# A hybrid encoder block: another way to build the row of c, a first scaled sum moved, the last quarters of two projections by token tile, the FFN input by blocks

## The chip, the cores and the metric

The kernel runs on one core of a Trainium2 chip. The metric is device time in microseconds (us) of one execution; lower is better. The core has a matrix engine (TensorE, PE in the profile; PEld is its weight load), a vector engine (DVE), a scalar engine (ACT), GpSimd (POOL) and SyncE (SP), which here only issues transfers. Each engine works through its own list of instructions in order. The lists are made ahead of time by a planner, which goes by program order as a priority, knows which instruction needs which, and hands out the buffers of a tag in program order; instructions wrapped in `order(...)` keep their written order on their engine whatever the planner would like better.

## What is computed

One layer on 256 tokens of width 2048, followed by an RMSNorm. The parts around the change:

```python
c_act = jax.nn.silu(c)
mod = c_act @ ada_w + ada_b
shift_m, scale_m, gate_m, shift_f, scale_f, gate_f = jnp.split(mod[:, None, :], 6, axis=-1)
h = rms_norm(x, norm_mix_w) * (1 + scale_m) + shift_m
proj = h @ w_in
...
x = x + gate_m * ((g_a * y_a + g_b * y_b) @ w_out)
hf = rms_norm(x, norm_ffn_w) * (1 + scale_f) + shift_f
gt, up = jnp.split(hf @ w_gate_up, 2, axis=-1)
x = x + gate_f * ((jax.nn.silu(gt) * up) @ w_down)
return rms_norm(x, norm_final_w)
```

Between the two lie a bidirectional mLSTM and a bidirectional gated delta rule, which the change leaves alone.

## The kernel before

All weights are streamed once from HBM in tiles of 1 MB, 128 partitions by 8 KB, into the tag `raw` of pool `st`, which has three buffers. Products of full precision are made from halves: `wh` is the weight rounded to the matmul's format (a copy on ACT, L165), `wl` the rest (a subtraction on DVE, L166), each with three buffers, and each product is three matmuls: high by high, low by high, high by low (L181 to L183).

**The opening.** `c` comes as one line of 8 KB; four row matmuls against ones spread it over the 128 partitions, and ACT takes its Silu into `row_c` (L100, L101). `cst` (which holds the identity, `ident`) and `pk` are loaded behind it on ACT's queue. The two token tiles `xt0` and `xt1` of x come on SP's queue, into the tag `ra` with five buffers, of which a third is taken by `junk`, the unused output of ACT's sums of squares (L417). 32 transposes on PE, in eight banks of four, turn x into feature blocks; DVE copies each bank (L424). Then sixteen blocks follow in a loop. Block b loads `ra0`, `ra1` (rows of the modulation weights, for scale and shift) and `raw` (input weights for sixteen output groups), in this order on SP. DVE multiplies `ra0` by `row_c` and sums it (L443), scales x with the sum and with `rows`, the tokens' reciprocal norms (L444), sums `ra1` likewise (L445); ACT adds that sum as a bias (L446) and rounds to `hh` (L447), DVE makes `hl` one block later (L450), and PE runs sixteen products of 256 columns (L452), of two passes each.

**The projections.** `tjob` runs a product by token tiles: chunks of four k blocks in halves of two; for each k block it serves token tile 0 and then 1, so both accumulators end together. `o` (output projection of the mixer) has four column groups of four chunks each, `d` (down projection) four groups of eleven chunks. When a group ends, `residual` multiplies by the gate row and adds to `x1` on DVE (L1008, L1009), and ACT sums the squares (L1010).

**The other modulation parts** are summed in the background: `ada_part` loads a 1 MB tile on SP, also into `raw`, and DVE multiplies and sums it (L110). `pump()`, called once per chunk, takes one such step at every second call in `o` (`every[0]`), every fourth in the FFN; `sums(P)` empties the list. Behind `o` it finishes part 4, which the FFN input needs.

**The FFN input.** `token_rstd` makes the reciprocal norms (L1014 to L1016). For each of four column quarters DVE scales both token tiles (`xn`, L1043), PE transposes (L1050), DVE applies scale and shift from PSUM (`hf`, L1052), and ACT and DVE split into `hfh` and `hfl`, two feature blocks at a time (L205, L206). Then eleven column groups run a gate job, an up job, and transposes of their product into `ffh` and `ffl`.

**The end.** After `d`, `token_rstd` again, then DVE scales x1 by token and by the final weight `nf` (L1092), group by group, each followed by its store on SP (L1093).

## Time and profile before

| | |
|---|---|
| runs | 2104.91, 2110.9, 2117.63 us; median 2110.9 |
| profiled execution | 2114.43 us, its span from first to last instruction 2112.6 us |
| mean granted TensorE clock | 0.984 |
| transfers | 485.64 MB, mean 230 GB/s |
| opening, to the end of its last block of products on PE | 0 to about 139 us |
| `o`, last quarter's last matmul | starts at 1345.58 us |
| gate, first matmul | starts at 1357.65 us |
| `d`, last matmul | starts at 2097.65 us |

A row of the timeline gives start and length in us, the engine (a q behind its name: its queue or sequencer), the line of the kernel, the operation, the tile written and the tiles read, the shape and a count if several were merged. In brackets stands how long the engine sat idle before it and which engine's instruction, or which transfer, ended that. A row of a window gives its length, the busy time of PE, PEld, DVE, ACT and POOL with instruction counts, the clock granted to PE as a share, the busy share of the transfer engines and GB/s. Matmuls are pipelined: one of 512 columns is shown with 0.39 us and starts 0.23 us after the one before.

### The profile page before, as it was taken

What the parts mean: (1) busy time and instruction counts of PE and PEld (TensorE: products, weight loads), DVE (VectorE), ACT (ScalarE), POOL (GpSimd) and SP (SyncE); (2) the same over time, 40 slices, a digit from 0 to 9 for tenths busy, and PEclk for the clock granted to TensorE, in tenths of its full rate; (3) what the DMA queues carried; (4) which work ended last, traced back from release to release, by engine and by line L of the source; (5) the groups of instructions that cost most, each with busy time, mean ns of one, the idle gap of its engine ahead of it and who ended that gap; (6) DMA issues with size and microseconds to landing.
All of it is one profiled execution on the core that took longest, in us unless ns stands there. A gap on an engine that the chain in (4) does not pass through costs nothing.

```text
span 2112.6 us, 26903 instructions
## 1 busy us (share of the span) xinstructions
PE 2034.2 (96%) x10374; PEld 1704.1 (81%) x10374; DVE 1403.3 (66%) x2065; ACT 1041.7 (49%) x1545; POOL 76.7 (4%) x149
## 2 busy tenths in 40 slices
PE   8999999989999899999999999899999999999997
PEld 6877779967988798888777878678888888878885
DVE  6788767776886687765677777765656654454454
ACT  2147557745773677555443444344444444444442
POOL 0002100100010000000000000000000000000000
PEclk9999999999999999999999999899999999999999
DMA  9976664456566656577986677666666665555553
GB/s 393 421 316 173 185 224 154 149 172 229 193 205 198 223 196 218 186 252 250 343 324 248 241 299 280 234 219 234 241 239 222 240 218 192 187 199 195 187 195 120
DMA packets 81075, 485.64 MB, mean 230 GB/s; under 512 B 9881, under 2 KB 19361, under 8 KB 26545
## 3 DMA queue, kind: packets, MB, share of 16 engines
q1 hardware_dynamic: 68672, 459.34, 60.3%
q0 software_dynamic: 4960, 9.49, 2.7%
q10 hardware_dynamic: 7314, 15.10, 1.9%
q8 instruction: 81, 1.33, 0.2%
q14 instruction: 48, 0.39, 0.1%
HBM read 467.07 MB, written 16.82 MB: 229 GB/s over the span
## 4 chain that ended last, share of the span: by engine, by line
PE 76%; DVE 8%; DMA 8%; issue 5%; ACT 3%; POOL 0%; SPq 0%; DVEq 0%; ACTq 0%; POOLq 0%
PE acc_up L183 4%; PE acc_up L181 4%; PE acc_up L182 4%; PE acc_d L181 4%; PE acc_d L182 4%; PE acc_d L183 4%; PE acc_gt L181 4%; PE acc_gt L182 4%; PE acc_gt L183 4%; PE first L452 3%; PE acc_b L145 2%; PE acc_b L147 2%; PE acc_b L146 2%; PE acc_o L181 2%; PE acc_o L182 2%
## 5 line engine op out<-in xcount | busy, mean ns | idle before, releaser
L166 DVE TENSOR_TENSOR wl_d<-raw_d,wh_d 128x1024 fp32r<-128x1024 f32 x88 | 107.8, 1225 | 123.2 <-ACT wh_d L165 123.2
L166 DVE TENSOR_TENSOR wl_up<-raw_up,wh_up 128x1024 fp32r<-128x1024 f32 x88 | 107.8, 1225 | 111.7 <-ACT wh_up L165 111.7
L110 DVE SCALAR_TENSOR_TENSOR ada<-ada,crow 128x2048 f32<-128x2048 f32 x64 | 146.3, 2286 | 43.8 <-DMA ada<-ada 43.4
L145 PE MATMUL acc_b<-hh,wh_b 128*128 128x256 f32 x576 | 163.8, 284 | 0.0
L147 PE MATMUL acc_b<-hh,wl_b 128*128 128x256 f32 x576 | 161.1, 280 | 1.8 <-DVE wl_b L142 1.8
L166 DVE TENSOR_TENSOR wl_gt<-raw_gt,wh_gt 128x1024 fp32r<-128x1024 f32 x88 | 107.1, 1224 | 83.7 <-ACT wh_gt L165 83.7
L165 ACT ACTIVATE wh_d<-raw_d 128x1024 fp32r<-128x1024 f32 x88 | 93.3, 1061 | 138.9 <-PE acc_d L182 134.0
L146 PE MATMUL acc_b<-hl,wh_b 128*128 128x256 f32 x576 | 160.2, 278 | 0.0
L165 ACT ACTIVATE wh_gt<-raw_gt 128x1024 fp32r<-128x1024 f32 x88 | 93.2, 1060 | 135.2 <-PE acc_gt L182 78.4
L165 ACT ACTIVATE wh_up<-raw_up 128x1024 fp32r<-128x1024 f32 x88 | 93.3, 1060 | 117.8 <-PE acc_up L182 84.7
L181 PE MATMUL acc_gt<-wh_gt,hfh 128*128 128x512 f32 x352 | 138.6, 397 | 2.9 <-ACT hfh L205 2.7
L182 PE MATMUL acc_gt<-wh_gt,hfl 128*128 128x512 f32 x352 | 139.3, 396 | 0.0
L183 PE MATMUL acc_gt<-wl_gt,hfh 128*128 128x512 f32 x352 | 138.5, 393 | 0.0
L181 PE MATMUL acc_d<-wh_d,ffh 128*128 128x512 f32 x352 | 137.5, 391 | 0.0
L182 PE MATMUL acc_d<-wh_d,ffl 128*128 128x512 f32 x352 | 137.5, 391 | 0.0
L183 PE MATMUL acc_d<-wl_d,ffh 128*128 128x512 f32 x352 | 137.0, 389 | 0.0
L181 PE MATMUL acc_up<-wh_up,hfh 128*128 128x512 f32 x352 | 137.0, 389 | 0.0
L183 PE MATMUL acc_up<-wl_up,hfh 128*128 128x512 f32 x352 | 137.0, 389 | 0.0
L182 PE MATMUL acc_up<-wh_up,hfl 128*128 128x512 f32 x352 | 137.0, 389 | 0.0
L452 PE MATMUL first<-x,raw 128*128 128x256 f32 x512 | 114.6, 386 | 6.6 <-ACT x L446 6.6
L452 PEld LDWEIGHTS first<-x,raw 128*128 128x128 f32 x512 | 98.3, 193 | 22.9 <-ACT x L446 9.4
L147 PEld LDWEIGHTS acc_b<-hh,wl_b 128*128 128x128 f32 x576 | 108.6, 189 | 2.2 <-DVE wl_b L142 2.2
(344 smaller groups left out, 5245.2 us busy)
## 6 DMA issues: line engine op xcount, KB each, us to landing
ada<-ada SPq DMA_DIRECT2D x64, 1024.0 KB, 4.9
raw_gt<-wgu SPq DMA_DIRECT2D x44, 1024.0 KB, 4.9
raw_up<-wgu SPq DMA_DIRECT2D x44, 1024.0 KB, 4.9
raw_d<-wd SPq DMA_DIRECT2D x44, 1024.0 KB, 4.8
raw_b<-winb SPq DMA_DIRECT2D x36, 1024.0 KB, 4.9
ra<-ada SPq DMA_DIRECT2D x32, 1025.0 KB, 14.6
raw<-win SPq DMA_DIRECT2D x16, 1024.0 KB, 12.7
raw_z<-wint SPq DMA_DIRECT2D x16, 1024.0 KB, 5.2
```

Of the source, the lines that this page charges most:

```text
L110: V.scalar_tensor_tensor(raw, raw, 1.0, row_c[:, :D], ALU.mult, ALU.mult, accum_out=mod[:, c0 + b : c0 + b + 1])
L145: PE.matmul(o, wh[:, k], hh[:, kk], start=kk == 0, stop=False)
L146: PE.matmul(o, wh[:, k], hl[:, kk], start=False, stop=False)
L147: PE.matmul(o, wl[:, k], hh[:, kk], start=False, stop=kk == KB - 1)
L165: order(S.activation(wh, raws[u][:, k0 : k0 + 2], AF.Copy), early)
L166: order(V.tensor_tensor(wl, raws[u][:, k0 : k0 + 2], wh.bitcast(F32), ALU.subtract), early)
L181: PE.matmul(ps[t], xh[:, kk, c], wh[:, k], start=kk == 0, stop=False)
L182: PE.matmul(ps[t], xl[:, kk, c], wh[:, k], start=False, stop=False)
L183: PE.matmul(ps[t], xh[:, kk, c], wl[:, k], start=False, stop=kk == last)
L452: PE.matmul(first[o], raw[:, o], x[:, b], start=b == 0 and o % 2 == 0, stop=b == KB - 1 and o % 2 == 1)
```

## The change

The row of c: `c` is loaded feature by partition (128 lines of 16 numbers), Silu is taken there, each of sixteen columns is spread over a tile of ones on DVE, transposed on PE and copied from PSUM by DVE. `junk` moves into `hl`. The loads of a block become a function and put `raw` ahead of the two `ra` from block 1 on; the first scaled sum of block 0 stands behind the first copy of x; ACT takes every second copy. `tjob` gets `last_by_token`: its last chunk runs all products of token tile 0, then of 1, with `done` called after each. The last groups of `o` and `d` use it, with their residuals in forced order. The background sums and an early square root (`root`, whose result nobody reads) come before the last group of `o`; another such root before the last group of `d`. The first gate job is a generator that is advanced from inside the last `o` group (its first half of weights) and from inside the FFN input, which now goes block by block. In `d`, the product with `nf` is taken group by group for the first three groups, and the last scaling is shared by DVE and ACT.

```diff
-    c1 = st.tile([1, D], F32, tag="raw", bufs=3, name="c1")
-    S.dma_start(c1, crow.unsqueeze(0))
+    cR = st.tile([P, KB, P], F32, tag="raw", bufs=3, name="cR")
+    S.dma_start(cF, crow)
...
+    order(S.activation(cF, cF, AF.Silu))
     for g in range(4):
         pc_ = acc_ps.tile([P, 512], F32, tag="acc", name=f"crow{g}")
-        PE.matmul(pc_, ones[0:1], c1[:, g * 512 : (g + 1) * 512], start=True, stop=True)
-        S.activation(row_c[:, g * 512 : (g + 1) * 512], pc_, AF.Silu)
+        for e in range(4):
+            b = 4 * g + e
+            order(V.tensor_scalar(cR[:, b], ones, cF[:, b : b + 1], None, ALU.mult))
+            order(PE.transpose(pc_[:, e * P : (e + 1) * P], cR[:, b], ident))
+        order(V.tensor_copy(row_c[:, g * 512 : (g + 1) * 512], pc_))
...
         todo = [(u, k0) for u in range(len(chunks)) for k0 in (0, 2)]
-        made = [halves(*q) for q in todo[:early]]
-        if early:
-            yield True
+        made = []
+        for i, q in enumerate(todo[:early]):
+            made.append(halves(*q))
+            if steps > 1 or i == early - 1:
+                yield True
...
+        if last_by_token:
+            w = [halves(len(chunks) - 1, k0) for k0 in (0, 2)]
+            for t in range(2):
+                c = slice(t * P, (t + 1) * P)
+                for k in range(4):
...
+                done(t, ps[t])
+                yield True
...
-        junk = w0.tile([P, D + 2], F32, tag="ra", bufs=5, name="junk")
+        junk = hl.rearrange("p b t -> p (b t)")[:, :D]
...
+        def loads(b):
+            ra = [w0.tile([P, D + 2], F32, tag="ra", bufs=5, name=f"ra{b}_{i}") for i in range(2)]
+            raw = st.tile([P, N0, P], F32, tag="raw", bufs=3, name=f"raw0_{b}")
+            if b:
+                order(nc.sync.dma_start(raw, win0[b]))
+            for i in range(2):
+                order(nc.sync.dma_start(ra[i], ada2[b, :, i]))
+            if not b:
+                order(nc.sync.dma_start(raw, win0[b]))
+            return ra, raw
...
-            V.tensor_copy(x[:, 2 * b2 : 2 * b2 + 2], px.rearrange("p (e t) -> p e t", e=2))
+            if b2 % 2:
+                order(S.activation(x[:, 2 * b2 : 2 * b2 + 2], pe_, AF.Copy))
+            else:
+                order(V.tensor_copy(x[:, 2 * b2 : 2 * b2 + 2], pe_))
+            if b2 == 0:
+                m2 = scale(0, ra)
...
+    gt0 = gate(0)
     for g in range(4):
...
+        job = tjob(f"o{g}", [wo[g, u] for u in range(4)], mgh, mgl, done_o, last_by_token=g == 3)
+        for i, _ in enumerate(job):
+            if g == 3 and i == 6:
+                next(gt0)
+        if g == 2:
+            sums(P)
+            root()
-    sums(P)
     background.append(ada_part(5, row_c))
-    every[0] = 4
+    every[0] = 0
...
+    def moved(b):
+        px = gps(f"pxn{b}")
+        for t in range(2):
+            f = b % 4 * P
+            order(PE.transpose(px[:, t * P : (t + 1) * P], xns[b // 4][:, t, f : f + P], ident))
+        hfs[b] = hp.tile([P, T], F32, tag="hf", bufs=2, name=f"hf{b}")
+        order(V.tensor_scalar(
+            hfs[b], px[:, 0:T], affn[:, b : b + 1], mod[:, 3 * KB + b : 3 * KB + b + 1], ALU.mult, ALU.add
+        ))
+        order(S.activation(hfh[:, b], hfs[b], AF.Copy))
+
+    def low(b):
+        order(V.tensor_tensor(hfl[:, b], hfs.pop(b), hfh[:, b].bitcast(F32), ALU.subtract))
+        if b == 1:
+            next(gt0)
+        if b % 2:
+            next(gt0)
+
+    normed(0, slice(0, P), V)
+    normed(0, slice(P, 512), S)
+    for b in range(KB):
+        moved(b)
+        if b:
+            low(b - 1)
+        if b % 4 == 2 and b < 12:
+            normed(b // 4 + 1, slice(0, 512), S)
+    low(KB - 1)
+    every[0] = 4
...
+        run(tjob(f"d{g}", [wd[g, u] for u in range(KD)], ffh, ffl, done_d, last_by_token=g == 3))
+        if g < 3:
+            for t in range(2):
+                V.tensor_tensor(x1[:, t, c], x1[:, t, c], nf[:, c], ALU.mult)
+        if g == 2:
+            root()
     rs = token_rstd(ss2, "rs2")
-    for g in range(4):
+    for g in (3, 0, 2, 1):
         c = slice(g * 512, (g + 1) * 512)
         for t in range(2):
-            V.scalar_tensor_tensor(x1[:, t, c], x1[:, t, c], rs[:, t : t + 1], nf[:, c], ALU.mult, ALU.mult)
+            if g == 3:
+                V.scalar_tensor_tensor(x1[:, t, c], x1[:, t, c], rs[:, t : t + 1], nf[:, c], ALU.mult, ALU.mult)
+            elif g == 2:
+                V.tensor_scalar(x1[:, t, c], x1[:, t, c], rs[:, t : t + 1], None, ALU.mult)
+            else:
+                S.activation(x1[:, t, c], x1[:, t, c], AF.Copy, scale=rs[:, t : t + 1])
```

In `normed(q, parts, eng)` both token tiles' columns of a quarter are scaled by the tokens' reciprocal norms, on DVE or ACT. `gate(j)` makes the gate job of group j with `early=2, steps=2` for j = 0, so all of its halves are in forced order and its first two are made one step at a time.

112 lines of the change are left out of this document (66 added, 46 removed).

## The prediction

> **What bounds the kernel now.** I read the page first, then the timeline of the three places that the diff touches (0 to 142 us, 1290 to 1388, 2095 to 2113), with the queue rows of SP and sums by window.
>
> ```profile
> PE 2034.2 (96%) x10374; PEld 1704.1 (81%) x10374; DVE 1403.3 (66%) x2065; ACT 1041.7 (49%) x1545; POOL 76.7 (4%) x149
> ```
>
> TensorE is busy 96% of 2112.6 us, so 78 us of idle is all that an edit around the matmuls can win, and the touched places hold only part of it. First the opening stage, from the timeline (start, length, then the row; in brackets what the engine waited for):
>
> ```profile
> 1.29 0.36 ACTq L85 DMA_DIRECT2D cst<-cst  x1
> 9.74 5.61 PE L423 MATMUL pxx<-cst,xt 128*128 128x128 f32 x32
> 9.85 0.60 ACT L101 ACTIVATE crow<-crow 128x512 f32<-128x512 f32 x1 [1.11 <-PE crow L100]
> 13.46 3.11 DVE L424 COPY x<-pxx 128x512 f32<-128x512 f32 x5 [0.16 <-PE pxx L423]
> 15.31 0.80 SPq L439 DMA_DIRECT2D ra<-ada  x2
> 17.07 2.35 DVE L443 SCALAR_TENSOR_TENSOR ra<-ra,pk,crow 128x2050 f32<-128x2050 f32 x1
> 19.93 2.29 DVE L445 SCALAR_TENSOR_TENSOR ra<-ra,crow 128x2050 f32<-128x2050 f32 x1
> 22.25 0.51 ACT L446 ACTIVATE x<-x,m 128x256 f32<-128x256 f32 x1 [3.87 <-DVE ra L445]
> 22.82 52.55 PE L452 MATMUL first<-x,raw 128*128 128x256 f32 x232 [4.85 <-ACT x L446]
> 32.23 0.33 SPq L440 DMA_DIRECT2D raw<-win  x1
> ...
> 111.27 2.35 DVE L443 SCALAR_TENSOR_TENSOR ra<-ra,pk,crow 128x2050 f32<-128x2050 f32 x1 [2.03 <-DMA ra<-ada]
> 118.73 2.35 DVE L443 SCALAR_TENSOR_TENSOR ra<-ra,pk,crow 128x2050 f32<-128x2050 f32 x1 [2.03 <-DMA ra<-ada]
> 131.99 7.17 PE L452 MATMUL first<-x,raw 128*128 128x256 f32 x32 [0.39 <-ACT x L446]
> ```
>
> The c row is whole at 10.45, both x tiles are released when the 32 transposes end (15.31, where SP issues the next ra), block 0 starts on PE at 22.82 and gives its raw buffer back at 32.23, 9.41 later. A later block takes PE 7.17, but they come every 7.46 us (118.73 - 111.27): three 1 MB loads per block, 2.49 us each, with DVE waiting for the ra. So the transfers bound the late blocks, and any time in which the queue runs dry is lost for good. It does so once today:
>
> ```profile
> 16.00:18.00 2.00, 0.67 (x2) 0.30 (x2) 1.97 (x5) 0.00 (x0) 0.00 (x0) 1.00 0.82 209
> 20.00:22.00 2.00, 0.00 (x0) 0.00 (x0) 2.00 (x2) 0.00 (x0) 0.00 (x0) 0.62 1.02 430
> 28.00:30.00 2.00, 2.00 (x11) 1.77 (x10) 1.99 (x2) 0.22 (x1) 0.00 (x0) 1.00 1.03 434
> ```
>
> In these windows (length, five engines' busy time, then granted clock, DMA share, GB/s) 209 against 430 GB/s is 1.0 us lost, which puts the first bytes of a new issue near 16.3, about 1 us behind the issue.
>
> **The opening, part by part.** The c row now needs the identity, which comes with cst; two more durations are needed:
>
> ```profile
> cst<-cst ACTq DMA_DIRECT2D x1, 198.5 KB, 7.6
> L423 PE MATMUL pxx<-cst,xt x32: 272/421/474, 9.7 to 15.1; 128*128 128x128 f32 x32
> 1257.73 0.87 DVE L997 TENSOR_SCALAR dg<-cst,mod 128x128 f32<-128x128 f32 x4 [0.46 <-PE row L999]
> ```
>
> cst lands at 1.29 + 7.6 = 8.9. Before that the new loads, Silu and four scalings are done (cF is 128 rows of 64 bytes; if it takes three times the 8 KB line it replaces, it is still there first). Then, group by group and in a forced order on DVE: four scalings 0.87, the last transpose 0.42 and two handovers of 0.05, the copy 3.11/5 = 0.62; 2.0 a group. The first group ends near 10.7 (its scalings were early), three more make 16.9. The eight pairs of x transposes now stand behind the c transposes on PE: they begin at 15.9; four banks hold them, and the bank of the third pair is emptied on DVE only behind the moved first scaling (17.6 to 20.0), so the last pair ends at 22. Of the removed work, PE's 7 us of row matmuls and ACT's four Silus win nothing, since nothing waits for them alone. DVE is through the copies at 22.5 (ACT takes every second); reciprocal and diagonal can slip into its waits. Then x times sum (0.45), the second sum 2.29, ACT 0.51: block 0 at 25.8, 3.0 late.
>
> Transfers: without the junk tile the fifth ra buffer is free, so seven tiles run ahead instead of five, up to 16.2 + 2 x 2.49 = 21.2; the next ra waits for an x tile until 22.1 and flows at 23.0, 1.9 dry. New too: from block 1 on raw is issued ahead of its two ra. raw of block 3 waits for block 0 on PE, now 25.8 + 9.4 = 35.2, and both ra of block 3, which today went ahead of it, stand behind that wait on SP. Four tiles are left in the queue, till 33.0; it is dry until 36.1. From there 13 blocks of three tiles make 97.1: the last ra is in at 133.7 (with 0.5 of landing), and it is now the last tile of all, so second sum, bias and hand-over (2.29 + 0.51 + 0.2) follow it: last block at 136.7 against 131.99, **+4.7**. PE alone would give 35.2 + 14 x 7.17 = 135.6. Bounds: today's last tile comes in two loads after the last first ra (118.73 + 7.46), at 131.2; with no dry queue at all it is 130.2, and the 3.0 behind it makes +1.2, so a gain is excluded. Reciprocal and diagonal not slipped in, and a later cst, make +7.
>
> **The last quarter of o.** Queue rows of SP around its start, rows of DVE, ACT and PE, and from the page the ada loads with their time to landing:
>
> ```profile
> 1307.39 2.54 SPq L162 DMA_DIRECT2D raw_o<-wo  x2
> 1312.77 0.33 SPq L109 DMA_DIRECT2D ada<-ada  x1
> 1318.21 2.54 SPq L162 DMA_DIRECT2D raw_o<-wo  x2
> 1323.65 0.33 SPq L109 DMA_DIRECT2D ada<-ada  x1
> ...
> 1318.10 2.28 DVE L110 SCALAR_TENSOR_TENSOR ada<-ada,crow 128x2048 f32<-128x2048 f32 x1
> 1318.58 1.06 ACT L165 ACTIVATE wh_o<-raw_o 128x1024 fp32r<-128x1024 f32 x1 [1.66 <-PE acc_o L182]
> 1321.30 1.06 ACT L165 ACTIVATE wh_o<-raw_o 128x1024 fp32r<-128x1024 f32 x1 [1.66 <-PE acc_o L182]
> 1345.58 0.39 PE L183 MATMUL acc_o<-wl_o,mgh 128*128 128x512 f32 x1
> ...
> ada<-ada SPq DMA_DIRECT2D x64, 1024.0 KB, 4.9
> ```
>
> A half chunk takes PE 2.72 us (1321.30 - 1318.58), a quarter eight of them, 21.8: the last quarter starts at 1345.97 - 21.8 = 1324.2. Its first load is the second issue of the 1307.39 row (1309.6); one ada load follows inside the quarter's first chunk, three more later. The change empties the ada sums before this quarter: four ada loads now stand ahead of its first weights, in the same three raw buffers and the same SP order. Shifted by one place the ada are issued at 1309.6, 1312.8, about 1317.8 and 1319; the quarter's first load needs the buffer of the second, which lands at 1317.6, waits on DVE for the sum before and a half, and is through at 1321.1; 4.9 to land makes 1326.0, wh 1.06 more: first matmul 1327.1, **+3.0** of stall. Bounds: 0 if loads keep today's order; 6 if the four sums (9.1 of DVE) also hold back the first wl, and PE restarts cold. What the cold costs is in the opening's windows: PE's last work before block 0 lies in 16 to 18, the clock is 0.62 in 20 to 22 and whole in 28 to 30, and block 0 takes 2.2 longer than a later one. The early root after the third quarter lies in ACT's idle (1.66 before each wh).
>
> The Trainium skill (TensorE: Matmul & The Clock Gate, What's actually happening) has the clock halved after an idle window of about 3.4 us; by that a 3.0 us stall escapes the 2.2 and one of 4 does not. The trace puts the drop 2 to 4 us after the last work and doesn't contradict it.
>
> **FFN input.** From the timeline:
>
> ```profile
> 1352.49 2.49 PE L1050 MATMUL pxn<-cst,xn 128*128 128x128 f32 x10 [6.52 <-DVE xn L1043]
> 1357.65 1.22 PE L181 MATMUL acc_gt<-wh_gt,hfh 128*128 128x512 f32 x2 [2.67 <-ACT hfh L205]
> 1373.55 0.69 DVE L206 TENSOR_TENSOR hfl<-hf,hfh 128x512 fp32r<-128x512 f32 x1 [0.70 <-ACT hfh L205]
> 1374.74 1.22 DVE L166 TENSOR_TENSOR wl_gt<-raw_gt,wh_gt 128x1024 fp32r<-128x1024 f32 x1
> 1375.87 0.54 DVE L1052 TENSOR_SCALAR hf<-pxn,affn,mod 128x256 f32<-128x256 f32 x1
> 1377.11 0.69 DVE L206 TENSOR_TENSOR hfl<-hf,hfh 128x512 fp32r<-128x512 f32 x1 [0.70 <-ACT hfh L205]
> 27.15 0.42 DVE L450 TENSOR_TENSOR hl<-x,hh 128x256 fp32r<-128x256 f32 x1
> ```
>
> Today the first gate matmul is 11.7 behind the end of o. Afterwards the first token tile's residual and square lie under the second tile's matmuls and are through 0.6 before that end; then, in the forced order, the early gate half (wh 1.06, wl 1.22) till +1.8, the second residual till +3.1 (no ada sum here any more), square, sum, root and reciprocal till +4.7, the first 128 columns and their transposes till +5.6, first hf and hfh till +6.8: 4.9 earlier. Then the pace: today a pair of blocks takes 3.56 (1377.11 - 1373.55). Afterwards DVE must do hf, low, hf, low, wl in that order, while on ACT the wh of a pair stands behind its second hfh, and wl behind wh. hf 0.46, low 0.38, hf 0.54, hfh 0.42, wh 1.06, wl 1.15 to the next start, three handovers: 4.1 a pair, 1.2 of it DVE waiting for wh. Six of eight pairs pay it (two halves are early): -4.9 + 6 x 0.54 = **-1.7**. Bounds: -8 if PE paced the pairs (12 matmuls and 4 transposes, 2.7 + 0.6 = 3.3), +1 if the early half waits for its weights and holds the second residual.
>
> **The end.**
>
> ```profile
> 2097.39 1.37 DVE L1008 TENSOR_TENSOR tmss<-acc_d,gf 128x512 f32<-128x512 f32 x2 [5.39 <-PE acc_d L183]
> 2100.75 1.28 ACT L1015 ACT_TABLE_LOAD   x1
> 2104.02 4.51 SPq L1093 DMA_DIRECT2D outT<-x  x4
> 2107.00:2109.00 2.00, 0.00 (x0) 0.00 (x0) 0.96 (x2) 0.00 (x0) 0.00 (x0) 0.50 1.01 384
> ```
>
> The early root takes the table load, 1.28, off the path (ACT has room for it in the last quarter), the token split about half of the double product, 0.4. Scaling in three places saves nothing: stores already run at a DMA share of 1.01 behind the first issue. **-1.7**, bounds -0.6 (early root undone by another load) and -2.2. The six extra products with nf hide in d's waiting DVE; uncovered they are 6 x 0.68.
>
> The Trainium skill (ScalarE: Activation LUTs, What ACT_TABLE_LOAD costs) counts 2.66 with a drain, which would make this -3.1. Here the root follows the load without a gap, so the row decides.
>
> Sum: 4.7 + 3.0 - 1.7 - 1.7 = +4.3. The profiled execution took 2114.4 (1.8 of it outside the span) and would take 2118.7; it lies 3.5 above the median of three, 2110.9, so the forecast is 2115.2, rounded 2115: slower, by less than can be told.
>
> **Rivals.** *Faster*: the schedule keeps o's loads ahead of the ada (0), the opening loses only its tail (+1.2), the FFN goes at 3.4 a pair (-4.9 - 8 x 0.16 = -6.2), the end -1.7: -6.7, 2104. For it speaks that PE idles 6.52 + 2.67 us at the FFN input; against it the order written for wh. *Clearly slower*: one mechanism, the starved last quarter. From a stall of 3 to 4 us on (the drop in the opening's windows), PE restarts at half clock while four sums fill DVE: 3.8 + 2.2 there, the rest as summed: +7.3, 2118; with the opening at its bound too it is 2121. For it: the three raw buffers; against: DVE could let halves pass between the sums. *It doesn't do what it says*: the scaled sum isn't sooner, since the c row ends at 16.9 instead of 10.45; that is in my sum. Elsewhere, a planner that reorders the untouched middle could move it by some 10 either way.
>
> **How the numbers follow.** Forecast 0.50 (its own range 2109 to 2120), faster 0.22, clearly slower 0.20, the middle reordered 0.08. The range to be held 8 times in 10 takes in the first two rivals and the spread of the three runs before (2104.9 to 2117.6): 2104 to 2124. A measurement here tells about 0.5% (10.6 us) from no change; below 2100.3 lies a quarter of the fast rival and part of the reordering, 0.09; above 2121.5 nearly half of the slow rival, half the reordering and a tenth of the forecast, 0.18; between them 0.73.
>
> **What would show it.** First block of the opening later than 25 us, a second dry stretch of DMA near 33 to 36, last block after 134.5; four ada issues in a row ahead of the last quarter and PE waiting for wh_o there; first gate matmul about 7 us behind o, then pairs slower than 3.9; no table load before the last root. I am wrong if the c row is done before 13 us, if the last quarter starts without a wait, or if gate pairs come every 3.3 us.

## The result: 36.7 us slower, and the profile after

| | before | after |
|---|---|---|
| median of the runs taken side by side | 2110.22 us (2104.91 to 2117.63) | 2146.91 us (2140.98 to 2150.82) |
| ratio, 95% interval | | 1.0158, 1.0135 to 1.0182 |
| span of the profiled execution | 2112.6 us | 2143.3 us |
| opening: span's start to the last block's first matmul | 132.0 | 141.4 |
| middle: from there to the third quarter of `o` (not touched) | 1170.3 | 1164.4 |
| third and last quarter of `o`, to its last matmul | 43.3 | 52.5 |
| FFN input: from there to the last matmul of the first up job | 62.7 | 82.0 |
| rest of FFN and `d`, to `d`'s last matmul | 689.3 | 689.4 |
| end: from there to the span's end | 15.0 | 13.6 |

The stages are differences of the starts that the trace gives for the named matmuls. Without the middle the touched stages add up to 9.4 + 9.2 + 19.3 + 0.1 - 1.4 = 36.6 us, close to the 36.7 between the medians, whose interval allows 28 to 38. The middle is 5.9 shorter in this profile, with the same code; it is not counted as an effect, for the reason given with the last experiment. The prediction said +4.3.

The first line of the page after: PE's busy time has grown, although the products are the same apart from the row of c, and its share has fallen.

```profile
PE 2043.8 (95%) x10382; PEld 1711.0 (80%) x10382; DVE 1406.6 (66%) x2085; ACT 1055.1 (49%) x1571; POOL 76.8 (4%) x149
```

**Opening, after**, from the timeline (start, length, engine, line, operation; idle time before in brackets):

```profile
16.48 0.69 DVE L106 COPY crow<-crow 128x512 f32<-128x512 f32 x1 [0.62 <-PE crow L105]
17.94 2.35 DVE L455 SCALAR_TENSOR_TENSOR ra<-ra,pk,crow 128x2050 f32<-128x2050 f32 x1
23.89 0.48 DVE L485 SCALAR_TENSOR_TENSOR x<-x,m,rows 128x256 f32<-128x256 f32 x1 [1.21 <-ACT rows L477]
27.18 30.42 PE L493 MATMUL first<-x,raw 128*128 128x256 f32 x128 [3.75 <-ACT x L487]
36.91 0.33 SPq L445 DMA_DIRECT2D raw<-win  x1
141.36 7.17 PE L493 MATMUL first<-x,raw 128*128 128x256 f32 x32 [0.29 <-ACT x L487]
```

The c row is whole at 17.2 instead of 10.45, so the first scaled sum, moved ahead in the text, starts at 17.94 instead of 17.07. DVE then sits idle 1.21 us for `rows`, and block 0 starts on PE at 27.18 instead of 22.82. SP can issue raw of block 3 only when block 0 gives its buffer back, at 36.91, with both ra of that block behind it. What that does to the transfers, by window (length, five engines' busy time, granted clock, transfer share, GB/s):

```profile
30.00:32.00 2.00, 2.00 (x6) 1.59 (x5) 2.00 (x4) 0.37 (x1) 0.00 (x0) 0.50 0.94 398
32.00:34.00 2.00, 2.00 (x10) 1.75 (x9) 2.00 (x1) 0.56 (x2) 0.00 (x0) 0.92 0.01 4
34.00:36.00 2.00, 2.00 (x11) 1.77 (x10) 1.97 (x4) 0.00 (x0) 0.00 (x0) 1.00 0.06 12
36.00:38.00 2.00, 2.00 (x11) 1.76 (x10) 1.28 (x3) 0.93 (x2) 0.00 (x0) 1.00 0.20 25
38.00:40.00 2.00, 2.00 (x11) 1.75 (x10) 0.00 (x0) 0.00 (x0) 0.00 (x0) 1.00 0.85 287
```

Against some 425 GB/s of a full window, 398, 4, 12, 25 and 287 are 6.6 us of lost transfers, in a stage that the transfers bound. The trace has the opening's last tile in at 138.13 where it was 131.24 before, 6.9 later; it is now a ra, behind which second sum, bias and handover take 3.23 to the last block's first matmul, where 0.75 lay behind the last raw. 6.9 and 2.5 are the 9.4.

**Last quarter of `o`, after**, from the timeline of SP, DVE, ACT and PE:

```profile
1313.70 8.98 SPq L114 DMA_DIRECT2D ada<-ada  x4
1322.62 2.29 DVE L115 SCALAR_TENSOR_TENSOR ada<-ada,crow 128x2048 f32<-128x2048 f32 x1 [0.30 <-DMA ada<-ada]
1324.95 11.37 SPq L167 DMA_DIRECT2D raw_o<-wo  x4
1326.36 2.29 DVE L115 SCALAR_TENSOR_TENSOR ada<-ada,crow 128x2048 f32<-128x2048 f32 x1 [1.44 <-DMA ada<-ada]
1328.58 1.28 DVE L1049 TENSOR_TENSOR tmss<-acc_o,gm 128x512 f32<-128x512 f32 x2
1330.49 0.63 ACT L1051 ACTIVATE tmss<-x 128x512 f32<-128x512 f32 x1 [10.05 <-DVE x L1050]
1331.83 1.99 ACT L170 ACTIVATE wh_o<-raw_o 128x1024 fp32r<-128x1024 f32 x2
1332.92 0.80 PE L190 MATMUL acc_o<-wh_o,mgh 128*128 128x512 f32 x1 [5.19 <-ACT wh_o L170]
1334.88 0.80 PE L192 MATMUL acc_o<-wl_o,mgh 128*128 128x512 f32 x1 [0.74 <-DVE wl_o L171]
```

The window behind it (length, five engines, granted clock, transfers):

```profile
1330.00:1340.00 10.00, 6.34 (x15) 4.61 (x16) 7.12 (x9) 5.25 (x9) 0.00 (x0) 0.66 0.88 322
```

Four ada loads go out in a row, the third only when DVE has summed the first; the quarter's first weights are issued at 1324.95, when the second is summed, and the trace has them landed at 1331.25. DVE takes the third quarter's residual (1328.58) only behind the third sum, ACT waits 10.05 for it, and `wh_o` comes behind that at 1331.83, 0.58 after the landing: nearly all of the wait is for the load. PE stands 5.19 us, then 0.74 more for `wl_o`, which stands behind the fourth sum on DVE, and restarts with a mean clock of 0.66.

**FFN input, after**, two of the eight pairs of blocks, and the sums of waits from 1320 to 1425 (engine and tile, what it waited for, total us, times, longest):

```profile
1374.07 0.39 PE L192 MATMUL acc_gt<-wl_gt,hfh 128*128 128x512 f32 x1
1374.30 0.60 PE L1134 MATMUL pxn<-cst,xn 128*128 128x128 f32 x4
1377.70 0.80 PE L190 MATMUL acc_gt<-wh_gt,hfh 128*128 128x512 f32 x1 [2.80 <-ACT wh_gt L170]
1378.29 0.63 PE L191 MATMUL acc_gt<-wh_gt,hfl 128*128 128x512 f32 x1
1378.72 0.63 PE L190 MATMUL acc_gt<-wh_gt,hfh 128*128 128x512 f32 x1
...
1381.90 0.60 PE L1134 MATMUL pxn<-cst,xn 128*128 128x128 f32 x4
1382.32 0.54 DVE L1136 TENSOR_SCALAR hf<-pxn,affn,mod 128x256 f32<-128x256 f32 x1 [3.42 <-PE pxn L1134]
1384.20 1.04 ACT L170 ACTIVATE wh_gt<-raw_gt 128x1024 fp32r<-128x1024 f32 x1
1385.30 0.50 PE L190 MATMUL acc_gt<-wh_gt,hfh 128*128 128x512 f32 x1 [2.80 <-ACT wh_gt L170]
1385.63 0.39 PE L191 MATMUL acc_gt<-wh_gt,hfl 128*128 128x512 f32 x1
...
1388.50 0.60 PE L1134 MATMUL pxn<-cst,xn 128*128 128x128 f32 x4
```

```profile
ACT hfh L1139 <- DVE hf L1136: 32.8, 15, 6.6
DVE hf L1136 <- PE pxn L1134: 21.0, 8, 4.8
...
PE acc_gt L190 <- ACT wh_gt L170: 15.9, 6, 2.8
```

The four transposes of the next pair start 0.23 us behind the last gate matmul of this one, every time: on PE they stand behind the products. DVE waits 3.42 for them, ACT waits for DVE, and PE waits 2.80 for `wh_gt`. It is one chain through three engines, in which PE does nothing while the others work: from 1381.90 to 1385.30 the transposes, two hf, two hfh and wh (3.40), then twelve matmuls to 1388.50 (3.20), together 6.60 for this pair where PE's own work is about 3.3. The pair before it took 7.60 (1374.30 to 1381.90), because some of its matmuls ran 0.43 us apart.

**The end, after**: ACT's root right behind DVE's sum, after 0.23 of idle and with no table load between, and the stores.

```profile
2132.49 0.29 ACT L1060 ACTIVATE rs<-rs,epsc 128x2 f32<-128x2 f32 x1 [0.23 <-DVE rs L1059]
2134.38 3.53 SPq L1204 DMA_DIRECT2D outT<-x  x4
```

### The profile page after: what moved, and what is told of

It reads as the page before. It is cut to its first block, busy times and chain, and to the rows that moved or that the text cites. A ratio compares the mean times of both kernels' runs of the same rounds, so it can differ in the third digit from the quotient of the medians.

```text
span 2143.3 us, 26972 instructions
## 1 busy us (share of the span) xinstructions
PE 2043.8 (95%) x10382; PEld 1711.0 (80%) x10382; DVE 1406.6 (66%) x2085; ACT 1055.1 (49%) x1571; POOL 76.8 (4%) x149
## 4 chain that ended last, share of the span: by engine, by line
PE 75%; DVE 9%; DMA 7%; issue 5%; ACT 3%; POOL 0%; SPq 0%; ACTq 0%; DVEq 0%; POOLq 0%
PE acc_gt L192 4%; PE acc_gt L190 4%; PE acc_gt L191 4%; PE acc_up L190 4%; PE acc_up L191 4%; PE acc_up L192 4%; PE acc_d L190 4%; PE acc_d L192 4%; PE acc_d L191 4%; PE acc_b L150 3%; PE acc_b L152 3%; PE acc_b L151 3%; DMA ra<-ada 2%; PE first L493 2%; PE acc_o L192 2%
## 5 line engine op out<-in xcount | busy, mean ns | idle before, releaser
L190 PE MATMUL acc_gt<-wh_gt,hfh 128*128 128x512 f32 x352 | 142.4, 405 | 16.0 <-ACT wh_gt L170 15.9
```

What stands on the lines that cost most here:

```text
L190: PE.matmul(ps[t], xh[:, kk, c], wh[:, k], start=kk == 0, stop=False)
```

## The experiments

Each kernel was timed beside the kernel before on the same chip; the median of the kernel before then lay between 2109.6 and 2113.1. Stage lengths are read as in the table above, from one profile each; the diffs are shortened, and the comments in them are added for the reader.

| kernel | median us | ratio to before, 95% interval | opening | o, two quarters | FFN input | end |
|---|---|---|---|---|---|---|
| the change | 2146.9 | 1.0158, 1.0135 to 1.0182 | 141.4 | 52.5 | 82.0 | 13.6 |
| e1_turns_ahead | 2125.6 | 1.0069, 1.0050 to 1.0088 | 141.8 | 52.6 | 61.1 | 13.6 |
| e2_ffn_before | 2130.8 | 1.0088, 1.0065 to 1.0111 | 142.5 | 52.6 | 64.2 | 13.6 |
| e3_sums_behind | 2140.6 | 1.0140, 1.0124 to 1.0157 | 141.6 | 43.3 | 80.9 | 13.6 |
| e4_opening_before | 2136.2 | 1.0120, 1.0103 to 1.0137 | 133.3 | 52.4 | 82.1 | 14.2 |
| e5_loads_before | 2142.7 | 1.0115, 1.0064 to 1.0166 | 134.8 | 51.3 | 79.9 | 13.6 |
| e6_crow_before | 2137.4 | 1.0109, 1.0069 to 1.0150 | 138.5 | 52.9 | 81.7 | 13.6 |
| e7_end_alone | 2111.7 | 0.9995, 0.9973 to 1.0017 | 133.0 | 43.3 | 63.2 | 13.6 |
| e8_mended (its z differs, see below) | 2110.0 | 0.9989, 0.9968 to 1.0010 | 132.9 | 45.2 | 54.4 | 14.1 |
| e9_mended_z_whole | 2102.5 | 0.9949, 0.9931 to 0.9966 | 131.7 | 43.3 | 54.7 | 13.6 |
| e10_halves_ahead | 2119.9 | 1.0031, 1.0016 to 1.0047 | 142.5 | 52.0 | 55.3 | 13.7 |
| e11_sums_spread | 2139.2 | 1.0130, 1.0110 to 1.0149 | 141.8 | 43.3 | 80.2 | 13.6 |
| e12_before_again | 2110.8 | 1.0003, 0.9981 to 1.0024 | 132.7 | 43.3 | 63.0 | 14.9 |

**The FFN input.** First the written order on PE alone: the transposes are issued three blocks ahead.

```diff
+    for b in range(3):
+        turn(b)
     for b in range(KB):
-        moved(b)          # transposes, hf, hfh
+        moved(b)          # hf, hfh
+        if b % 4 == 0 and b < 12:
+            normed(b // 4 + 1, slice(0, 512), S)
+        turn(b + 3)       # transposes of block b + 3
         if b:
             low(b - 1)
-        if b % 4 == 2 and b < 12:
-            normed(b // 4 + 1, slice(0, 512), S)
```

> The changed kernel with one thing moved: in the FFN input the transposes of a block are issued three blocks ahead, so on PE they stand in front of the gate matmuls of the current pair instead of behind them (the scaling of a quarter comes two blocks earlier for that). Theory A (order on PE: each pair's transposes wait behind 12 gate matmuls, so transposing, scaling, rounding, weight half and matmuls follow one another): pairs fall from 6.6-9 us to about 4.1, the end of the gate job comes 17 to 21 us earlier, total 2126 to 2130. Rival B (the weight half behind the second rounding on ACT alone makes the chain): pairs stay above 6, total within 4 us of 2147. Rival C (PE's half clock is the cause, not the order): matmuls still cold, gain under 8 us.

Measured: 21 us off the FFN input (82.0 to 61.1) and off the time (2146.9 to 2125.6). The pairs, by DVE's weight halves:

```profile
1381.79 1.23 DVE L171 TENSOR_TENSOR wl_gt<-raw_gt,wh_gt 128x1024 fp32r<-128x1024 f32 x1 [2.32 <-ACT wh_gt L170]
1385.89 1.22 DVE L171 TENSOR_TENSOR wl_gt<-raw_gt,wh_gt 128x1024 fp32r<-128x1024 f32 x1 [1.10 <-ACT wh_gt L170]
1389.98 1.23 DVE L171 TENSOR_TENSOR wl_gt<-raw_gt,wh_gt 128x1024 fp32r<-128x1024 f32 x1 [1.10 <-ACT wh_gt L170]
```

They come every 4.1 us, with 1.10 of DVE waiting for wh: the pace that the prediction had worked out, and the stage is 1.6 shorter than before the change. So the written order, with the transposes on PE behind the products, cost the 21 us. (The scaling of the next quarter moved two blocks ahead with them, as they need it.)

Then the whole FFN input as in the kernel before (its code and the gate job back, `every[0] = 4`; the sums stay ahead of the last quarter).

> The changed kernel with the FFN input and the first gate job as before (two feature blocks at a time, gate weights not advanced from inside it, background sums on), all else changed. Theory A: the FFN input costs the change 19 us, of which the early start of the chain gives little back: total 2126 to 2130, and from the last matmul of o to the first up group the same as before. If the loss arises in the last quarter of o or later in the FFN instead, total stays above 2140.

```diff
-        run(gate(j) if j else gt0)
+        run(tjob(f"gt{j}", [wgu[j, 0, u] for u in range(4)], hfh, hfl,
+                 lambda ps: [S.activation(sg[:, t], ps[t], AF.Silu) for t in range(2)]))
```

It comes out 3.1 us behind e1_turns_ahead in the FFN input, and its time a little above the 2126 to 2130 expected. That does not compare the two forms alone: its first gate matmul stands 9.2 behind `o` (7.1 in e1_turns_ahead), and one background sum of 2.28 lies inside the stage. What each of these makes of the 3.1 was not tested.

The last step takes the other wait out too: wh of pair p + 1 is made on ACT before hfh of the block that follows, its wl on DVE one step before its matmuls. Everything else is as in the change; the diff is against e1_turns_ahead.

```diff
         for u, k0 in todo:
+            if ahead:
+                n = todo.index((u, k0)) + 1
+                nxt = high(*todo[n]) if n < len(todo) else None   # wh of the next pair
+                yield True
+                if nxt:
+                    made.append(rest(*nxt))                       # its wl
             wh, wl = made.pop(0) if made else halves(u, k0)
...
     for b in range(KB):
+        if b and b % 2 == 0:
+            next(gt0)
         moved(b)
-        if b % 4 == 0 and b < 12:
-            normed(b // 4 + 1, slice(0, 512), S)
+        if b % 2 == 0 and b < 12:
+            f = b % 4 * P
+            normed(b // 4 + 1, slice(f, f + 2 * P), S)
```

> The changed kernel with the FFN input alone rearranged: transposes three blocks ahead of the gate matmuls (as in e1_turns_ahead) and besides each pair's wh made a pair ahead and its wl one step before its matmuls. The prediction priced 4.1 us a pair by 'wh stands behind the second hfh', and e1_turns_ahead ran at 4.1. Theory A (that chain on ACT and DVE is the pace): with the halves ahead, PE sets it, 12 matmuls of 0.227 and 4 transposes of 0.15 make 3.3; pairs at 3.3 to 3.5, from o's end to up0's end 8 to 9 us shorter than before the change (27 to 28 shorter than in the changed kernel), 5 to 7 shorter than e1_turns_ahead; median 2118 to 2121. Theory B (DVE's own work and handovers): pairs 3.9 or more and the median that of e1_turns_ahead, 2125.

Measured 2119.9, and 55.3 for the stage, 5.8 less than in e1_turns_ahead. From its timeline:

```profile
1378.18 1.23 DVE L174 TENSOR_TENSOR wl_gt<-raw_gt,wh_gt 128x1024 fp32r<-128x1024 f32 x1
1381.30 1.23 DVE L174 TENSOR_TENSOR wl_gt<-raw_gt,wh_gt 128x1024 fp32r<-128x1024 f32 x1
```

The window of the stage:

```profile
1370.00:1396.00 26.00, 26.00 (x120) 21.31 (x119) 23.09 (x39) 19.79 (x37) 0.00 (x0) 0.92 0.48 162
```

No wait is left before wl, pairs take 3.1 us, PE is busy the whole 26.00 us and DVE 23.09 of them. Theory A holds: the pairs come a little faster than it said (3.3 to 3.5), and the stage is 7.4 shorter than before the change where it said 8 to 9.

**The last quarter of `o`.** First the sums back behind `o`:

```diff
         if g == 2:
-            sums(P)
             root()
+    sums(P)
     background.append(ada_part(5, row_c))
```

> The changed kernel with the background sums emptied behind the last quarter of o again (the early root stays). Theory A (four ada loads ahead of the quarter's first weights starve PE, then it restarts cold): PE runs from the third quarter into the last without a stall, that place is 7 to 9 us shorter, total 2138 to 2140. Rival D (the wh of the last quarter waits on ACT behind the squares of the residual and the root, not for its load): the stall stays, total within 3 us of 2147. A cost that comes back: the rest of the sums now delays the norm behind o by 2 to 3 us.

The two quarters take 43.3, as before the change: the stall is gone, with the last quarter still by token. The time fell less, by 6.4, and lies above the 2138 to 2140 expected. In its profile the middle took 1168.9 where the change's took 1164.4, with the same instructions up to `o`; the last experiment comes back to that. What held `wh_o` up was the load: with ACT's squares and the root still ahead of it, PE no longer waits there. A second way to the same end, two of the four sums moved ahead one by one:

```diff
         for i, _ in enumerate(job):
             if g == 3 and i == 6:
                 next(gt0)
+            if g in (1, 2) and i == 3:
+                sums()
         if g == 2:
-            sums(P)
             root()
+    sums(P)
```

> The changed kernel with the background sums alone moved: none are emptied ahead of the last quarter of o; two of them go into the second and third quarter (one more each), the rest follow every second chunk and behind o. Last quarter by token and early root stay. Theory A (the four ada loads in a row ahead of the quarter's first weights are the stall): the third and last quarter together take 43 to 45 us from first to last matmul as in the kernel before (43.3; 52.5 in the changed kernel), no PE wait above 1.5 us at wh_o, clock whole through the quarter; the FFN stretch stays as slow as in the changed kernel (19 us more than before); median 2137 to 2139. Theory B (the change of the quarter's order, by token, with the gate half inside it, is the stall): at least 5 of the 9.2 us stay; median 2142 or more.

Again 43.3, with PE busy and its clock whole across the last quarter:

```profile
1324.00:1346.00 22.00, 22.00 (x99) 18.22 (x98) 17.80 (x21) 10.77 (x15) 0.00 (x0) 1.00 0.84 310
```

So the four loads in a row are the stall, and the order by token costs nothing that can be read.

**The opening.** Whole as before (loads, c row, copies, first sum, junk), the rest as changed; beside the two edits shown further down:

```diff
-        junk = hl.rearrange("p b t -> p (b t)")[:, :D]
+        junk = w0.tile([P, D + 2], F32, tag="ra", bufs=5, name="junk")
...
-            if b2 == 0:
-                m2 = scale(0, ra)
```

> The changed kernel with the whole opening as before (row of c by matmuls, junk tile, ra ahead of raw, first sum in the loop). Theory A: block 0 at 22.8 and the last block at 132 again, 9.4 us earlier there; later stages had given back 4 of it by the end of the mixer, so the total gains 5 to 9, 2138 to 2142. Rival: the give-back is planner noise of the middle, then the gain is anywhere between 0 and 9 and the middle's order differs from both kernels'.

8.1 us of the opening come back, 10.7 in the time (2136.2, where 2138 to 2142 was expected); the last block stands at 133.3 where the kernel before has it at 132.0 to 133.0 in three profiles of the same opening. Two more kernels split it. Only the load order back:

```diff
-            if b:
-                order(nc.sync.dma_start(raw, win0[b]))
             for i in range(2):
                 order(nc.sync.dma_start(ra[i], ada2[b, :, i]))
-            if not b:
-                order(nc.sync.dma_start(raw, win0[b]))
+            order(nc.sync.dma_start(raw, win0[b]))
```

> The changed kernel with one thing undone: in the opening, each block's two ra tiles are issued ahead of its raw again, as before the change; the c row by transposes stays. Theory A (both c row and load order cost): with raw first, both ra of block 3 stand on SP behind the wait for block 0's end (36.9 us), and the transfers run dry from 32 to 38. With ra ahead, buffers that are free let ra tiles fill that hole: the dry stretch shrinks from 5.7 us to under 2, and the last block starts where PE itself sets it, 36.9 + 14 x 7.17 = 137.3, or 136 to 138 against 141.4; the rest of the kernel as in the changed kernel; median about 2143 (changed 2147). Theory B (the late block 0 alone does it; raw of block 3 waits for block 0 in either order): last block stays at 140 to 142, median 2146 to 2147.

The first and the last stretch of the opening's products on PE:

```profile
27.73 91.74 PE L490 MATMUL first<-x,raw 128*128 128x256 f32 x416 [3.75 <-ACT x L484]
...
134.82 7.17 PE L490 MATMUL first<-x,raw 128*128 128x256 f32 x32 [0.53 <-ACT x L484]
```

SP's issues there, from the timeline of its queue:

```profile
27.16 2.60 SPq L445 DMA_DIRECT2D ra<-ada  x2
36.62 0.33 SPq L446 DMA_DIRECT2D raw<-win  x1
```

And a window:

```profile
32.00:34.00 2.00, 2.00 (x11) 1.77 (x10) 2.00 (x4) 0.92 (x2) 0.00 (x0) 1.00 1.00 422
```

Block 0 is as late as in the change, and raw of block 3 is issued as late (36.62); but two ra go out at 27.16, ahead of the wait, and the transfers run on through 32 to 34 at 422 GB/s. The last block starts at 134.8, earlier than theory A had it (136 to 138): 2.8 behind the kernel before instead of 9.4. What is left is lost earlier. From 18 to 24 the three windows of 2 us move 111, 66 and 308 GB/s, which is 3.7 us lost where the kernel before lost 1.0, because the next ra is issued only at 20.54, behind the scaled sum of block 0 (18.16 to 20.5), and that waits for the row of c. And only the c row back, raw still first:

```diff
-        for e in range(4):
-            b = 4 * g + e
-            order(V.tensor_scalar(cR[:, b], ones, cF[:, b : b + 1], None, ALU.mult))
-            order(PE.transpose(pc_[:, e * P : (e + 1) * P], cR[:, b], ident))
-        order(V.tensor_copy(row_c[:, g * 512 : (g + 1) * 512], pc_))
+        PE.matmul(pc_, ones[0:1], c1[:, g * 512 : (g + 1) * 512], start=True, stop=True)
+        S.activation(row_c[:, g * 512 : (g + 1) * 512], pc_, AF.Silu)
```

> The changed kernel with one thing undone: the row of c comes from one line of 8 KB by four matmuls against ones and Silu on ACT, as before; load order (raw first), junk in hl, first scaled sum early and the shared copies stay. Theory A: the c row is whole at 10.5 instead of 17.2; block 0 starts at about 22.5 to 24 (27.2 changed, 22.8 before); raw of block 3 still waits for its end, but seven tiles had been issued ahead and only about 2 us go dry; last block at 134 to 137 against 141.4; median about 2141. Theory B (the c row is not what is late, the x copies behind ACT's squares and the moved sum are): block 0 stays after 25.5 and the last block after 139.

The same two of this kernel:

```profile
23.02 30.31 PE L489 MATMUL first<-x,raw 128*128 128x256 f32 x128 [3.75 <-ACT x L483]
...
138.47 7.17 PE L489 MATMUL first<-x,raw 128*128 128x256 f32 x32 [0.67 <-ACT x L483]
```

Its windows in which the transfers thin out:

```profile
30.00:32.00 2.00, 2.00 (x11) 1.76 (x10) 1.96 (x3) 0.00 (x0) 0.00 (x0) 1.00 0.50 205
32.00:34.00 2.00, 2.00 (x11) 1.75 (x10) 2.00 (x2) 0.00 (x0) 0.00 (x0) 1.00 0.49 74
34.00:36.00 2.00, 2.00 (x11) 1.77 (x10) 0.90 (x3) 0.92 (x2) 0.00 (x0) 1.00 0.73 295
```

The time of 2137.4 is below the 2141 expected. Block 0 starts at 23.0, as theory A said, and yet the last block only at 138.5, later than theory A had it (134 to 137). 205, 74 and 295 of 425 GB/s are 3.3 us lost though block 0 is not late at all. The last tile is in at 135.24, 4.0 later than before, and the last block's first matmul again 3.23 behind it; 4.0 and 2.5 are the 6.5. In e5_loads_before it is in at 134.08 (2.8 later) and 0.74 ahead of that matmul. So of the opening's 9.4, about 6.5 belong to raw first and about 2.8 to the late c row, and the two add within the 1 us by which this stage moves between profiles of the same opening (141.4 to 142.5 in six). The moved sum and the shared copies were not undone alone; the two parts leave nothing for them that can be read.

**The end alone**, on the kernel before (last quarter of `d` by token, root ahead of it, products with `nf` per group, shared scaling):

```diff
+        run(tjob(f"d{g}", [wd[g, u] for u in range(KD)], ffh, ffl, done_d, last_by_token=g == 3))
+        if g < 3:
+            for t in range(2):
+                V.tensor_tensor(x1[:, t, c], x1[:, t, c], nf[:, c], ALU.mult)
+        if g == 2:
+            root()
...
-    for g in range(4):
+    for g in (3, 0, 2, 1):
```

> The kernel before with the end part of the change alone: last column group of d by token tile, early root ahead of it, products with nf per group, last scaling shared by DVE and ACT. The opening, o and the FFN input are as before. Theory A: from d's last matmul to the span's end 13.5 to 13.7 us against 15.0, the table load off the path; everything else as before; median 1.4 below the kernel before, 2109 to 2111 (ratio 0.999), not to be told from no change in the time, but in the trace. Theory B: the six more products with nf and the forced order of the residuals hold up d's weight halves on DVE, and d takes 2 to 4 us longer.

The end takes 13.6, 1.4 less, and the stage with `d` is not longer (689.4). The time cannot tell it: 0.9995.

**A version against both kernels.** The opening as before with junk in `hl`, the sums spread as in e11_sums_spread, the FFN input as in e10_halves_ahead, the last quarters by token and the end as changed.

> A version meant to beat both: opening as before but with junk in hl (a fifth ra buffer free); the background sums not emptied ahead of the last quarter of o but two more of them spread over the second and third quarter; last quarter by token and early root kept; FFN input by blocks with transposes three blocks ahead of the gate matmuls AND each pair's wh made a pair ahead, its wl one step before its matmuls; end as changed. Theory A (order of issue is what cost the time): opening -1 to 0 against before (last block 131 to 132); last quarter of o without a stall; first gate matmul 7 us behind o, then pairs every 3.3 to 3.5 us instead of 4.1, so the stretch from o's end to up0's end 6 to 8 us shorter than before; end -1.4; median 2101 to 2104, ratio 0.995 to 0.997. Theory B (pairs are paced by something else, DVE's 3.1 us of work with its handovers): pairs stay at 3.9 to 4.1, the median is 2106 to 2109.

In e8_mended the first group of z, in the middle of the kernel, took, from its fourth step on, weight halves made for earlier steps, because it makes three of them early through the same code; so its time (2110.0, where 2101 to 2104 was expected) is not that of the whole computation. The next kernel gives the added step to the gate job alone:

```diff
-            if early:
+            if ahead:
                 n = todo.index((u, k0)) + 1
...
-early=0 if j else 1)
+early=0 if j else 1, ahead=not j)
```

> The version of e8_mended with the products of z made as in the kernel before (there, the first group of z took its weight halves in another order); the opening as before with junk in hl, sums spread over the second and third quarter of o, last quarter by token, FFN input with transposes three blocks ahead and halves a pair ahead, end as changed. Theory A: what e8_mended showed outside z holds: from o's end to up0's end 8 us shorter than in the kernel before, the last quarter of o without a stall (within 1.5 us of before), the end 1.4 shorter, the opening within 1.5 us of before; together 7 to 9 us; median 2102 to 2106 where the kernel before has 2111 to 2113, ratio 0.9955 to 0.998. Theory B (part of e8_mended's gain was its differing z): the stretches behind o are 4 us or less ahead of before, ratio 0.9985 or more.

Measured 2102.5 us beside 2112.7, ratio 0.9949 (0.9931 to 0.9966): faster than the kernel before by 10 us and than the change by 44. Its stages stand at 131.7, 43.3, 54.7 and 13.6; the FFN input brings 8.0 and the end 1.4, the opening nothing that can be told.

**The kernel before once more**, with no edit, for the spread of stages that nobody touched:

> The kernel before itself, profiled once more, to see how far stages move from one execution to the next where nothing is changed. Theory A (the untouched middle's 4 us less in the changed kernel's profile, and the 2 to 9 us less or up to 2 us more in other runs, are spread between executions): its stages outside the middle and the first quarter of o stay within 1 us of the first profile (opening's last block 132, last quarter of o 21.7, o's end to up0's end 62.7, end 15.0), while the middle or the first quarter of o moves by 2 to 9 us; ratio 1.00 within 0.003. Theory B (the stages are the same from run to run, and the changes move the middle): every stage within 1 us of the first profile.

From the last block of the opening to the first product of `o` it took 1114.6 in place of 1120.3, and the first quarter of `o` 34.0 in place of 28.2; every other stage agrees within 0.7. Those two differences cancel, so this run alone does not explain the change's 5.9: the middle of the table is 1170.3 both times. Other profiles do. The change, e1_turns_ahead, e2_ffn_before, e3_sums_behind and e10_halves_ahead have the same instructions and loads in the same order up to the first product of `o`, and their middle lies between 1159.7 and 1168.9. So the 5.9 is not counted as an effect. The planner did put part of the middle, between about 140 and 225 us, in another order in the kernels with raw first: 56 of PE's 6124 instructions between the opening and `o` stand elsewhere. The middles of the seven profiles with that order (1159.7 to 1168.9) overlap with those of the six with the old one (1163.0 to 1176.8), so an effect of a few us is neither shown nor excluded. What makes the middle move was not looked into.

## Why the prediction was wrong, step by step

The touched stages came 32.3 us above the sum of +4.3: 21.0 of that in the FFN input, 6.2 in the last quarter of `o`, 4.7 in the opening, and 0.4 behind.

**FFN input: the step that failed.** The prediction put it as "DVE must do hf, low, hf, low, wl in that order, while on ACT the wh of a pair stands behind its second hfh ... 4.1 a pair", and -1.7 with a worst case of +1. It followed the order on DVE and on ACT and never wrote down PE's; its sum has the next transposes done in time, as if they passed the products that they do not need. In the trace they stand behind them: the next pair's transposes come after twelve matmuls that wait for wh and wl. What was worked out as a pace of overlapped engines became one chain of 6.6 us and more: 82.0 against 62.7, +19.3. Of that PE's idle at `wh_gt` is 15.9, and part of the rest is matmuls 0.43 us apart after such waits (1378.29 to 1378.72) in place of 0.23. e1_turns_ahead, which changes only this, ran at 4.1 a pair and -1.6, so the rest of the sum for this stage was sound. The first gate matmul stood 6.7 behind the end of `o`'s last matmul (6.8 said), 5.0 earlier than before (4.9 said). The bound of -8 does not follow from its own terms: -4.9 and eight pairs at 3.3 for 3.56 make -7.0.

**Opening: the mechanism right, the sum too small (4.7 said, 9.4 measured).** The c row was whole at 17.2 (16.9 said, though three groups of 2.0 behind 10.7 make 16.7) and block 0 started at 27.18 (25.8): the reciprocal did not slip into DVE's waits, which the upper bound had allowed for. The dry stretch was seen ("dry until 36.1"), but began at 32 rather than 33 and ended past 38: 6.6 us lost, not 3.1. With two shorter stalls of the same kind, which the sum did not have (raw of blocks 4 and 7 landed 3.44 and 3.11 behind the tile ahead of them, where 2.49 is usual), the last tile, put at 133.7, was in at 138.13; the tail of 3.0 behind it was right (3.23). The prediction also made the load order's price a consequence of the late block 0, by which undoing the c row alone would have brought most of it back; e6_crow_before shows 6.5 from the load order with block 0 on time. The upper bound of +7 did not hold.

**Last quarter of `o`: the mechanism right, too small (3.0 said, 9.2 measured).** The first weights were put at 1321.1 and went out at 1324.95, but the third quarter itself starts 3.5 later after the change (1305.81 for 1302.29), so the chain of buffers and sums up to that issue was worked out to 0.3 us. What it had too small came behind: the load took 6.30 to land, not 4.9, with the ada loads still under way ahead of it, and then ACT's squares held `wh_o` up for 0.58. With the 0.74 for `wl_o`, which only the upper bound had, that makes 5.9 of waiting (5.19 and 0.74). The cold restart, which the prediction kept for a rival at 2.2 ("starved last quarter"), came on top: the first thirteen matmuls, up to 1339.70, took 3.1 longer than at 0.23 apart. So the rival's mechanism was the true one, and its 3.8 and 2.2 were still 3.2 short of the 9.2. The bound of 6 did not hold either. The Trainium skill (TensorE: Matmul & The Clock Gate, What's actually happening) has the clock halved after an idle window of about 3.4 us; after 5.19 us of idle the trace agrees, with matmuls at 0.80 and a mean clock of 0.66.

**End: right** (-1.7 said, -1.4 measured, e7_end_alone the same alone): no table load before the root, stores behind the first scaling.

**The rivals.** That the scaled sum would not come sooner was right (17.94 against 17.07). A reordered middle did occur in a small part, but it is no part of the loss: the middle came out 5.9 shorter, which lies within its spread. The fast rival's pace in the FFN (3.4 a pair) is possible, as e10_halves_ahead shows with 3.1, but not in the order that the change wrote. All signs that were to show the forecast right came: a first block later than 25, a second dry stretch, four ada issues in a row, pairs slower than 3.9, no table load. They said which way each stage would move and set no upper limit, so a pair of 6.6 passed as well as one of 4.1.

## What to carry to other kernels

Where an order is written out by hand, write down each engine's list, that of PE too, and ask of every instruction what stands ahead of it that it does not need: a transpose that feeds the next step belongs ahead of products that wait for this one, and a weight half a step before its use. Loads for background work go one at a time between the loads that the next products need; a row of them cost its transfers, its sums and a cold restart together here. In a stage that the transfers bound, what matters of a queue is which issue waits for a buffer and what stands behind it: here the tile whose buffer comes free last belonged last.

## What was not expected of the hardware

The clock of PE does not drop after a fixed idle time. In the FFN input after the change, the same idle of 2.80 us is followed once by matmuls at half pace (the one at 1377.70 is shown with 0.80 and the next with 0.63) and once at full pace (1385.30, and 0.39 for the one behind). The windows of the trace (length, five engines' busy time, granted clock, transfers) show where the difference lies:

```profile
1373.80:1377.20 3.40, 1.10 (x7) 0.69 (x6) 1.75 (x4) 1.33 (x3) 0.00 (x0) 1.00 0.00 0
1377.20:1380.60 3.40, 2.90 (x7) 2.33 (x8) 1.23 (x1) 1.67 (x3) 0.00 (x0) 0.50 0.00 0
1387.40:1390.80 3.40, 1.70 (x10) 1.20 (x8) 1.75 (x4) 0.73 (x2) 0.00 (x0) 1.00 0.95 308
```

From 1371 to 1414 the clock is half from 1377.2 to 1380.6, from 1397.7 to 1404.5 and from 1407.9 to 1411.3 and whole between, so its changes lie multiples of 3.4 us apart. In the stretches of 3.4 us ahead of the three drops PE was busy 1.10, 1.51 and 0.70; those between 1380.6 and 1394.2, with 1.70 to 2.23, were followed by a whole clock. So an idle of 2.80 costs the clock when enough of it falls into one such stretch (2.3 of it before 1377.2), and not when it is split more evenly over two (1.5 and 1.3 around 1384.0). The Trainium skill (the section named above) has a free-running window of about 3.4 us, by which the phase decides, and the trace agrees. A whole idle window was not needed here: one with 1.51 of work in it was enough, and the trace's numbers stand.

The other surprise is the spread of the untouched parts: in two executions of the same kernel the stretch up to the first product of `o` and the first quarter of `o` differ by 5.7 and 5.8 us in opposite directions, and the whole middle by nothing (1170.3 both times).
